# Down projections: a third weight block added in flight, and the seventh product's sums fetched later

## The chip, the cores and the metric

The kernel runs on one core of one Trainium2 chip. Its time is the device time of one execution in microseconds (us), and a smaller time is better. A profiled execution adds a trace: every instruction of the engines PE (matrix products; its weight loads are shown as PEld), DVE, ACT and POOL, the issues of the DMA queue SP, and the transfers' landings. Times inside the trace count from the start of its span.

## What is computed

One decoder layer on 512 rows of 1024 float32 values:

```python
x = x + 0.5 * swiglu(rmsnorm(x, ffn1_norm), ffn1_wg, ffn1_wu, ffn1_wd)
x = x + hybrid_mixer(rmsnorm(x, mix_norm), ...)     # sparse attention beside a gated recurrence
x = x + 0.5 * swiglu(rmsnorm(x, ffn2_norm), ffn2_wg, ffn2_wu, ffn2_wd)
return rmsnorm(x, final_norm)

def swiglu(x, w_gate, w_up, w_down):
    return (jax.nn.silu(x @ w_gate) * (x @ w_up)) @ w_down
```

The inner width of both feed-forward parts is 2816, so each down projection multiplies 512 x 2816 by 2816 x 1024. The change touches only the two down projections.

## The kernel before

Every float32 operand is split into a rounded part and a remainder, and each product is made of three matmuls. For weights this is `wsplit`: ACT writes the rounded part `wh`, and DVE subtracts it from the source to get the remainder `wl`. A step of PE cannot begin before both are there. The tiles `wh` and `wl` have three buffers each, and each holds the split weights of two steps, so the split of a step is placed four steps ahead of the step that uses it.

Of the 22 row blocks of a down weight, six (`PLAIN`) are multiplied directly. The other 16 form eight pairs (`PAIRS`), and for them the kernel uses a Strassen-like scheme with seven products instead of eight. Products 1, 2 and 4 multiply a block of the weight as it is. Products 5, 6, 3 and 7 multiply sums of two, three or four blocks, and these sums of weights are made anew in each execution:

- the sum for product 5 is block 2 + block 3,
- for product 6 it is block 2 + block 3 + block 0,
- for product 3 it is all four blocks,
- for product 7 it is block 2 + block 0.

The first three live one after the other in the same tile `sums[j]`: once product 5's split has read it, a block is added for product 6, and once that split has read it, another is added for product 3. In the first down projection these tiles are called `sm` in the profile, in the second they are the tiles `x`. Product 7's sums have tiles of their own, `s3[j]`, shown as `s`.

A sum is made in two ways. An *adding transfer* is a DMA issued by POOL (`G.dma_start(..., accum_op=ALU.add)`), which adds a block from memory to what the tile holds. The other way, used before for product 6 alone, fetches the block into a tile `a1` (shown as `a`, one of the four buffers of the pool `tmp`) through the queue SP, and DVE adds the two tiles.

`block_down` writes the order of the work out by hand. `steps` is the list of 68 steps of PE, and `task(i, f)` puts the function `f` behind the products of step `i`:

| steps | what |
|---|---|
| 0 to 5 | direct products of the first output half, k = 0 to 5 |
| 6 to 13, 14 to 21, 22 to 29 | products 1, 2 and 5 for the pairs j = 0 to 7 |
| 30 to 39 | product 6, with direct steps of the second half at 33 and 37 |
| 40 to 49 | product 3, with direct steps at 43 and 47 |
| 50 to 57, 58 and 59 | product 7, then the last two direct steps |
| 60 to 67 | product 4 |

A direct step is 12 matmuls with 512 moving columns. A step of products 1 to 7 is 12 matmuls with 256 columns in the first down projection, and 6 matmuls with 512 columns in the second. Each engine and each DMA queue works through its own instructions in the order in which they were written; the program does not reorder them. A transfer of POOL or SP that waits for a tile therefore holds all later transfers of the same queue.

Between the two feed-forward parts stands the mixer. Its order is not written by hand: a planner (`Plan`) keeps an account of the time of each engine, by a cost for each instruction, and places an instruction when its inputs are due by that account. The account begins with the first down projection (`plan.clear()`), so it takes in that projection's DVE additions and DMA issues too.

Of the kernel before, what the change touches and what calls it, by code (L numbers as in the profile page):

```python
# [12 lines left out]
ALU = mybir.AluOpType  # L13
# [161 lines left out]
def hybrid_kernel(ctx, tc, xt, vec, w1u, w1d, wm, wki, wrg, watt, wrnn, wout, w2u, w2d, gf, out):  # L175
    nc = tc.nc
    plan = Plan()
    V, A = plan.engine("DVE", nc.vector), plan.engine("ACT", nc.scalar)
    G, T = plan.engine("POOL", nc.gpsimd), plan.engine("PE", nc.tensor)
    Q = plan.engine("SP", nc.sync)  # L180
# [16 lines left out]
    def nm(s):  # L197
        cnt[0] += 1
        return f"{s}_{cnt[0]}"

    def slot(dt=F32, name="s"):
        return plan.take("slot", big.tile([P, S], dt, tag="slot", name=nm(name)))

    def work(name="t", cols=S):
        return plan.take("tmp", tmp.tile([P, cols], F32, tag="tmp", name=nm(name)))
# [28 lines left out]
    def wsplit(r, h, l):  # L234
        A.activation(h, r, AF.Copy)
        V.tensor_sub(l, r, f(h))
# [355 lines left out]
    def block_down(hs, wd, sums):  # L592

        d = Down()
        steps = [("D", 0, k) for k in range(PLAIN)] + [(p, j) for p in (1, 2, 5) for j in range(PAIRS)]  # L600
        for p in (6, 3):
            for j in range(PAIRS):
                steps += [(p, j)] + [("D", 1, (6, 3).index(p) * 2 + j // 3)] * (j in (2, 5))
        steps += [(7, j) for j in range(PAIRS)] + [("D", 1, k) for k in (4, 5)] + [(4, j) for j in range(PAIRS)]
        index = {s: i for i, s in enumerate(steps)}
        tasks = {}

        def task(i, *fs):
            tasks.setdefault(i, []).extend(fs)

        def block(b, j):

            i, half = b * (PAIRS // 2) + j // 2, j % 2 * S
            return wd[i][:, half:half + S]

        units, turned, ra, raws, s3, ones = {}, {}, {}, {}, {}, {}

        def fetch(key, i):
            def load():
                raws[key] = raw.tile([P, WMAX], F32, tag="raw", name=nm("wr"))  # L620
                Q.dma_start(raws[key], wd[i])

            return load

        def unit(i, src):
            def split_():
                if i % 2 == 0:
                    units[i // 2] = [wsp.tile([P, WMAX], F32R, tag=t, name=nm(t)) for t in ("wh", "wl")]
                wsplit(src(), *(t[:, i % 2 * S:(i % 2 + 1) * S] for t in units[i // 2]))

            return split_

        a = lambda j: hs[PLAIN + 2 * j]
        b = lambda j: hs[PLAIN + 2 * j + 1]

        def differences(j):
            def subs():
                if j % 2 == 0:
                    ra[j // 2] = slot(F32, "cr")
                V.tensor_sub(ra[j // 2][:, (lo, hi)[j % 2]], a(j)[:, hi], b(j)[:, hi])  # L640
                V.tensor_sub(a(j)[:, hi], a(j)[:, hi], a(j)[:, lo])

            return subs

        SRC = {1: lambda j: a(j)[:, lo], 5: lambda j: a(j)[:, hi], 6: lambda j: a(j)[:, lo], 3: lambda j: b(j)[:, hi],
               7: lambda j: ra[j // 2][:, (lo, hi)[j % 2]], 4: lambda j: a(j)[:, lo], 2: lambda j: b(j)[:, lo]}

        def operand(p, j):
            def make():
                o, src = slot(F32R, "cm"), SRC[p](j)  # L650
                turned[p, j] = o
                sign = -1.0 if p in (1, 3) else 1.0
                A.activation(o[:, lo], src, AF.Copy, scale=sign)
                if sign < 0:
                    V.scalar_tensor_tensor(o[:, hi], src, -1.0, f(o[:, lo]), op0=ALU.mult, op1=ALU.subtract)
                else:
                    V.tensor_sub(o[:, hi], src, f(o[:, lo]))

            return make

        used = []
        for i, st in enumerate(steps):
            if st[0] == "D":
                _, h, k = st
                key = ("D", h, k // 2)
                if k % 2 == 0:
                    used.append([i - 4, index["D", h, k + 1] - 4, key, 2 * PAIRS + h * (PLAIN // 2) + k // 2])
                task(i - 4, unit(i, lambda key=key, k=k: raws[key][:, k % 2 * S:(k % 2 + 1) * S]))
                continue
            p, j = st  # L670
            if p in (1, 4, 2):
                key = (p, j // 2)
                if j % 2 == 0:
                    used.append([i - 4, index[p, j + 1] - 4, key, {1: 0, 2: 1, 4: 3}[p] * (PAIRS // 2) + j // 2])
                src = lambda key=key, j=j: raws[key][:, j % 2 * S:(j % 2 + 1) * S]
            elif p == 7:
                src = lambda j=j: s3[j]
            else:
                src = lambda j=j: sums[j]
            if p == 1:  # L680
                task(j, differences(j))
            if p == 5:
                def base(j=j):
                    Q.dma_start(sums[j], block(2, j))

                def add(j=j):
                    G.dma_start(sums[j], block(3, j), accum_op=ALU.add)

                task(3 * j // 2 + 2, base)
                task(3 * j // 2 + 4, add)  # L690
            if p == 7:
                def base(j=j):
                    s3[j] = slot(F32, "s3")
                    Q.dma_start(s3[j], block(2, j))

                def add(j=j):
                    G.dma_start(s3[j], block(0, j), accum_op=ALU.add)

                task(i - 27, base)
                task(i - 25, add)  # L700
            if p == 6:
                def one(j=j):
                    ones[j] = work("a1")
                    Q.dma_start(ones[j], block(0, j))

                def second(j=j):
                    V.tensor_add(sums[j], sums[j], ones[j])

                task(i - 9, one)
                task(i - 5, second)  # L710
            if p == 3:
                def fourth(j=j):
                    G.dma_start(sums[j], block(1, j), accum_op=ALU.add)

                task(index[6, j] - 3, fourth)
            before = {1: 6, 6: 6, 7: i - j - 1, 4: i - index[3, j]}.get(p, 5)
            if p == 6:
                task(i - before - 1, lambda j=j: V.tensor_sub(a(j)[:, lo], b(j)[:, hi], a(j)[:, hi]))
            if p == 4:
                task(i - before - 1, lambda j=j: V.tensor_sub(a(j)[:, lo], b(j)[:, lo], a(j)[:, lo]))  # L720
            task(i - before, operand(p, j))
            task(i - 4, unit(i, src))
        used.sort()
        for n, (first, last, key, i) in enumerate(used):
            at = first - 5
            if n >= RAWS:
                at = max(at, used[n - RAWS][1])
            assert at < first
            task(at, fetch(key, i))

        def tasks_at(i):
            for t in tasks.pop(i, ()):
                t()

        d.steps, d.index, d.tasks, d.tasks_at, d.units, d.turned = steps, index, tasks, tasks_at, units, turned
        return d
# [52 lines left out]

    sums = []  # L790
    d1 = block_down(hs, w1d, sums)
    ffn_up(y, w1u, 2, hs, V_G1, ((WP[0], WP[1]), (WP[2], pu)), AH[1:], d1.tasks_at)

# [77 lines left out]
    steps, index, last = d1.steps, d1.index, len(d1.steps) - TAIL  # L871
# [689 lines left out]


    d2 = block_down(hs, w2d, x)
    steps, index, units, turned, tasks_at = d2.steps, d2.index, d2.units, d2.turned, d2.tasks_at
    xr = []
# [210 lines left out]
```

## Time and profile before

| | |
|---|---|
| median of 3 runs | 1078.01 us (1077.62 to 1078.6) |
| the profiled execution, its own time | 1076.99 us |
| its span in the trace | 1074.9 us |
| granted clock of TensorE, mean | 0.998 |
| PE busy | 1063.3 us, 99% of the span |
| DVE busy | 857.6 us, 80% |
| ACT busy | 657.5 us, 61% |
| POOL busy | 140.8 us, 13% |

The profiled execution is 1.02 us below the median, and 2.09 us of its time lie outside the span. The first down projection takes the stretch from about 235 to 350 us, the second that from about 946 us to the end. Matmuls overlap in the trace: one with 512 columns is shown as 0.39 us long but the next begins 0.23 us after it. So the busy share of PE hides short waits, and the distance between the starts of matmuls shows them.

### The profile page before, as it was taken

The page shows a single profiled execution, that of the slowest core. Times are in us where ns is not written, and L with a number is a line of the kernel's source. Part 1 is how long each engine was busy: PE and PEld are TensorE (multiplying, and loading weights), DVE is VectorE, ACT ScalarE, POOL GpSimd, SP SyncE. Part 2 cuts the span into 40 slices and gives each one's busy share as a digit, 9 for nine tenths or more (in the row PEclk, how much of TensorE's full clock was granted, in tenths as well). Part 3 has the DMA queues.
Part 4 walks back from the last instruction along what each step waited for, and adds up shares of the span by engine and source line. Part 5 has one row for each costly group of instructions (what it writes and reads, how often), then busy time and mean ns, then how long its engine had stood idle before and what let it go on. Part 6 is the DMA issues. An engine that isn't in the chain of part 4 may idle for free.

```text
span 1074.9 us, 17584 instructions
## 1 busy us (share of the span) xinstructions
PE 1063.3 (99%) x6412; PEld 945.4 (88%) x6412; DVE 857.6 (80%) x1668; ACT 657.5 (61%) x1297; POOL 140.8 (13%) x171
## 2 busy tenths in 40 slices
PE   9999999999999999999999999999999999999997
PEld 7889999999989778888888888888899999998776
DVE  6687777779988878998899867666878777778886
ACT  6565655555556658877896664345755555565563
POOL 0161111102320000000000000002511111101310
PEclk9999999999999999999999999999999999999999
DMA  7297677639983442332232213434977777549953
GB/s 276 65 255 194 162 190 196 165 110 242 238 196 118 139 124 83 94 98 79 79 99 82 76 38 86 131 99 128 236 181 192 166 190 191 123 133 285 231 134 118
DMA packets 71702, 161.79 MB, mean 151 GB/s; under 512 B 8512, under 2 KB 14784, under 8 KB 71616
## 3 DMA queue, kind: packets, MB, share of 16 engines
q1 hardware_dynamic: 48912, 123.92, 35.5%
q0 software_dynamic: 22272, 36.19, 20.5%
q8 instruction: 50, 0.82, 0.3%
q10 hardware_dynamic: 432, 0.57, 0.1%
q14 instruction: 36, 0.29, 0.1%
HBM read 151.73 MB, written 2.10 MB: 143 GB/s over the span
## 4 chain that ended last, share of the span: by engine, by line
PE 87%; DMA 6%; DVE 4%; ACT 2%; issue 1%; SPq 0%; POOL 0%; POOLq 0%; ACTq 0%; DVEq 0%
PE mm L169 60%; PE aux L169 26%; DVE wl L169 1%; DMA sm<-w1d 1%; DMA x<-w2d 1%; DMA s<-w2d 1%; DMA s<-w1d 1%; ACT wh L169 1%; DMA cm<-cb 1%; DMA x<-xt 0%; DMA wr<-w1u 0%; DVE yl L169 0%; DVE yf L169 0%; DVE ca L169 0%; ACT cm L169 0%
## 5 line engine op out<-in xcount | busy, mean ns | idle before, releaser
L169 PE MATMUL mm<-cm,wh 128*128 128x256 f32 x1472 | 268.6, 283 | 0.5 <-ACT wh L169 0.5
L169 DVE TENSOR_TENSOR wl<-wr,wh 128x512 fp32r<-128x512 f32 (+2 forms) x228 | 188.9, 832 | 77.9 <-ACT wh L169 77.0
L169 PEld LDWEIGHTS mm<-cm,wh 128*128 128x128 f32 x1472 | 230.1, 192 | 1.4 <-ACT wh L169 0.7
L169 PE MATMUL mm<-cm,wl 128*128 128x256 f32 x736 | 208.5, 283 | 0.2 <-DVE wl L169 0.2
L169 ACT ACTIVATE wh<-wr 128x512 fp32r<-128x512 f32 (+3 forms) x230 | 167.9, 737 | 62.1 <-issue 21.1
L169 PE MATMUL mm<-yh,wh 128*128 128x512 f32 (+1 forms) x416 | 164.2, 396 | 0.4 <-ACT wh L169 0.2
L169 PE MATMUL mm<-yl,wh 128*128 128x512 f32 (+1 forms) x416 | 162.5, 391 | 0.8 <-DVE yl L169 0.8
L169 PE MATMUL aux<-cm,wh 128*128 128x256 f32 x880 | 161.8, 283 | 0.1
L169 PE MATMUL mm<-yh,wl 128*128 128x512 f32 x408 | 159.3, 390 | 0.0
L169 PEld LDWEIGHTS mm<-cm,wl 128*128 128x128 f32 x736 | 141.3, 192 | 0.5 <-DVE wl L169 0.4
L169 PEld LDWEIGHTS aux<-cm,wh 128*128 128x128 f32 x880 | 137.3, 192 | 0.3 <-DMA cm<-cb 0.3
L169 PE MATMUL aux<-cm,wl 128*128 128x256 f32 x440 | 124.5, 283 | 0.0
L169 DVE TENSOR_TENSOR wl<-s,wh 128x512 fp32r<-128x512 f32 x152 | 104.0, 686 | 23.6 <-ACT wh L169 21.6
L169 ACT ACTIVATE wh<-s 128x512 fp32r<-128x512 f32 x152 | 92.5, 623 | 38.9 <-DVE s L169 30.9
L169 PEld LDWEIGHTS mm<-yh,wh 128*128 128x128 f32 (+1 forms) x416 | 77.9, 187 | 17.2 <-ACT wh L169 1.1
L169 PEld LDWEIGHTS mm<-yl,wh 128*128 128x128 f32 (+1 forms) x416 | 77.6, 187 | 16.9 <-DVE yl L169 2.2
L169 PEld LDWEIGHTS mm<-yh,wl 128*128 128x128 f32 x408 | 76.6, 188 | 16.5 <-DVE wl L169 0.2
L169 PEld LDWEIGHTS aux<-cm,wl 128*128 128x128 f32 x440 | 84.5, 192 | 0.0
L169 PE MATMUL mm<-wh,cm 128*128 128x512 f32 x192 | 59.6, 392 | 1.2 <-ACT wh L169 1.1
L169 ACT ACTIVATE tg<-mm 128x256 f32<-128x256 f32 x68 | 26.1, 384 | 52.8 <-PE mm L169 52.6
L157 POOL DMA_DIRECT2D cm<-cb x8 | 7.1, 886 | 334.6 <-DMA wr<-w2u 280.1
L157 POOL DMA_DIRECT2D s<-w2u x36 | 33.6, 1092 | 127.5 <-DMA s<-w2u 92.1
(243 smaller groups left out, 2016.8 us busy)
## 6 DMA issues: line engine op xcount, KB each, us to landing
wr<-wm SPq DMA_DIRECT2D x39, 512.0 KB, 3.5
wr<-w2u SPq DMA_DIRECT2D x26, 512.0 KB, 4.9
wr<-w1u SPq DMA_DIRECT2D x21, 512.0 KB, 5.9
wr<-w1d SPq DMA_DIRECT2D x18, 512.0 KB, 4.2
s<-w2u SPq DMA_DIRECT2D x36, 256.0 KB, 5.9
s<-w2u POOLq DMA_DIRECT2D x36, 256.0 KB, 5.0
wr<-w2d SPq DMA_DIRECT2D x18, 512.0 KB, 4.7
s<-w1u SPq DMA_DIRECT2D x32, 256.0 KB, 6.2
```

Of the source, the lines that this page charges most:

```text
L157: return self.engine.dma_start(out, src, **kw)
L169: return call(*args, **kw)
```

## The change

Three things are edited in `block_down`, and they act in both down projections:

- Product 6's third block is no longer fetched into `a1` and added by DVE. It is an adding transfer of POOL into `sums[j]`, written one step behind product 5's split of the same tile (step 19 + j) where the addition stood five steps ahead of product 6's step.
- Product 7's two transfers into `s3[j]` move from 27 and 25 steps ahead of its step to 14 and 12 ahead. The order on POOL's queue becomes: all eight additions for 6, all eight for 3, all eight for 7. Before, those for 7 alternated with those for 3.
- The dictionary `ones` and the tile `a1` go.

```diff
-        units, turned, ra, raws, s3, ones = {}, {}, {}, {}, {}, {}
+        units, turned, ra, raws, s3 = {}, {}, {}, {}, {}
...
                 def add(j=j):
                     G.dma_start(s3[j], block(0, j), accum_op=ALU.add)
 
-                task(i - 27, base)
-                task(i - 25, add)
+                task(i - 14, base)
+                task(i - 12, add)
             if p == 6:
-                def one(j=j):
-                    ones[j] = work("a1")
-                    Q.dma_start(ones[j], block(0, j))
-
                 def second(j=j):
-                    V.tensor_add(sums[j], sums[j], ones[j])
-
-                task(i - 9, one)
-                task(i - 5, second)
+                    G.dma_start(sums[j], block(0, j), accum_op=ALU.add)
+
+                task(index[5, j] - 3, second)
             if p == 3:
                 def fourth(j=j):
                     G.dma_start(sums[j], block(1, j), accum_op=ALU.add)
```

In each down projection SP loses eight fetches, DVE loses eight additions, and POOL's queue gets eight transfers more.

## The prediction

> **What bounds the kernel now.** The page comes first: its span and busy times.
>
> ```profile
> span 1074.9 us, 17584 instructions
> PE 1063.3 (99%) x6412; PEld 945.4 (88%) x6412; DVE 857.6 (80%) x1668; ACT 657.5 (61%) x1297; POOL 140.8 (13%) x171
> ```
>
> PE is the bound, so only time in which PE falls behind its own pace can be won. The pace is read next, in the timeline of PE, at the starts of direct steps (`aux<-hh` or `aux<-wh,hh`). First down projection, steps 33, 37, 43 and 47:
>
> ```profile
> 290.53 0.40 PE L169 MATMUL aux<-hh,wh 128*128 128x512 f32 x1
> ...
> 297.59 0.40 PE L169 MATMUL aux<-hh,wh 128*128 128x512 f32 x1
> ...
> 307.53 0.40 PE L169 MATMUL aux<-hh,wh 128*128 128x512 f32 x1
> ...
> 315.99 0.40 PE L169 MATMUL aux<-hh,wh 128*128 128x512 f32 x1
> ```
>
> From 33 to 37, one direct step and three others take 7.06 us. From 37 to 43, with five others, it is 9.94, so two others cost 2.88: 1.44 each, 2.74 for the direct one. From 43 to 47 stands the mix of the first stretch again, and it takes 8.46: PE loses 1.40 there. Second projection, steps 30, 33, 37, 43 and 47:
>
> ```profile
> 1003.81 0.62 PE L169 MATMUL mm<-wh,cm 128*128 128x512 f32 x2
> ...
> 1008.20 0.40 PE L169 MATMUL aux<-wh,hh 128*128 128x512 f32 x1
> ...
> 1016.61 0.39 PE L169 MATMUL aux<-wh,hh 128*128 128x512 f32 x1
> ...
> 1026.16 0.39 PE L169 MATMUL aux<-wh,hh 128*128 128x512 f32 x1
> ...
> 1035.06 0.39 PE L169 MATMUL aux<-wh,hh 128*128 128x512 f32 x1
> ```
>
> All matmuls have 512 columns here. From 37 to 43 stand 12 + 5 x 6 = 42 of them in 9.55 us, 0.227 each, which I take as the pace. The stretch from 30 to 33 (18 matmuls, 4.09) takes 4.39, from 33 to 37 (30 matmuls, 6.82) 8.41, from 43 to 47 (30 again) 8.90. The losses are 0.30, 1.59 and 2.08, 3.97 together. Both projections lose 1.40 + 3.97 = 5.37 us, in products 6 and 3 alone. What ends these waits is told by the timeline of ACT, whose last bracket is the idle time and its releaser:
>
> ```profile
> 1005.75 0.63 ACT L169 ACTIVATE wh<-x 128x512 fp32r<-128x512 f32 x1 [1.44 <-DVE x L169]
> ...
> 1030.00 0.63 ACT L169 ACTIVATE wh<-x 128x512 fp32r<-128x512 f32 x1 [1.50 <-DMA x<-w2d]
> ```
>
> ```profile
> 313.28 0.63 ACT L169 ACTIVATE wh<-sm 128x512 fp32r<-128x512 f32 x1 [1.46 <-DMA sm<-w1d]
> ```
>
> In product 6 of the second projection ACT waits for DVE's addition. With the addition 0.69 long, the rounding 0.63 and the subtraction 0.69,
>
> ```profile
> 1004.95 0.69 DVE L169 TENSOR_TENSOR x<-x,a 128x512 f32<-128x512 f32 x1
> ...
> 1006.42 0.69 DVE L169 TENSOR_TENSOR wl<-x,wh 128x512 fp32r<-128x512 f32 x1 [0.44 <-ACT wh L169]
> ```
>
> a block goes DVE, ACT, DVE in 2.01 us, longer than the 1.36 (6 x 0.227) of the step that it feeds. In product 3 the adding transfer itself lands late. Why is seen on POOL:
>
> ```profile
> 1021.10 0.87 POOL L157 DMA_DIRECT2D s<-w2d  x1 [2.24 <-DMA s<-w2d]
> 1021.63 3.01 POOL L157 DMA_DIRECT2D x<-w2d  x3
> ```
>
> The last three additions for product 3 (`x`) go out only after an addition for product 7 (`s`), which had to wait for its own base block. The windows of the two stages show the engines that carry the change:
>
> ```profile
> 300.00:319.00 19.00, 18.25 (x126) 16.70 (x125) 14.70 (x35) 10.91 (x25) 4.10 (x6) 1.00 0.90 212
> 319.00:334.00 15.00, 15.00 (x124) 14.87 (x123) 14.35 (x29) 11.40 (x22) 1.55 (x3) 1.00 0.19 55
> ...
> 1006.00:1020.00 14.00, 13.78 (x55) 9.44 (x54) 11.80 (x23) 6.27 (x13) 6.72 (x8) 1.00 1.06 256
> 1020.00:1035.00 15.00, 14.04 (x58) 10.38 (x58) 11.19 (x24) 8.45 (x21) 3.55 (x4) 1.00 1.01 228
> 1035.00:1052.00 17.00, 17.00 (x76) 14.05 (x76) 16.93 (x36) 11.26 (x25) 0.00 (x0) 1.00 0.17 59
> ```
>
> The columns are the stretch, its length, busy time of PE, PEld, DVE, ACT and POOL, PE's clock, the DMA engines' share and GB/s. The clock is 1.00 throughout, so there is none to win. DMA is full until product 7 begins and then nearly idle.
>
> **The change part by part.** *DVE's additions go.* Eight of 0.69 us in each projection, 5.5 us of DVE work, of which PE feels only the chain above: 0.30 + 1.59 = 1.89 us in the second projection. In the first, product 6 already runs at pace, so nothing is won there.
>
> *The addition becomes a transfer.* It has to land before ACT and DVE split the block. It can go out once DVE has read the tile for product 5. The first and the last of these eight subtractions in each projection:
>
> ```profile
> 271.94 0.68 DVE L169 TENSOR_TENSOR wl<-sm,wh 128x512 fp32r<-128x512 f32 x1
> ...
> 280.83 0.68 DVE L169 TENSOR_TENSOR wl<-sm,wh 128x512 fp32r<-128x512 f32 x1
> ```
>
> ```profile
> 990.89 0.69 DVE L169 TENSOR_TENSOR wl<-x,wh 128x512 fp32r<-128x512 f32 x1
> ...
> 999.75 0.69 DVE L169 TENSOR_TENSOR wl<-x,wh 128x512 fp32r<-128x512 f32 x1
> ```
>
> First projection: out at 272.6. Step 30 begins three steps before 290.53, at 286.2; a split of 0.63 + 0.68 makes 284.9 the last moment. That is 12.3 us. Second: from 991.6 to 1003.81 - 1.3 = 1002.5, 10.9 us. The eighth has 19 us in both (281.5 to 300.5; 1000.4 to 1019.4). The trace has no such transfer at this place; the nearest are the adding transfers of the same stages, and below them those of the second up projection:
>
> ```profile
> sm<-w1d POOLq DMA_DIRECT2D x16, 256.0 KB, 8.2
> ```
>
> ```profile
> x<-w2d POOLq DMA_DIRECT2D x16, 256.0 KB, 9.0
> ...
> s<-w2d SPq DMA_DIRECT2D x8, 256.0 KB, 9.2
> s<-w2d POOLq DMA_DIRECT2D x8, 256.0 KB, 9.9
> ```
>
> ```profile
> s<-w2u POOLq DMA_DIRECT2D x36, 256.0 KB, 5.0
> ```
>
> Medians from issue to landing are 8.2 and 9.0 at the upper end, 5.0 at the lower. All are under 10.9, so no wait takes the place of the old one. I expect about 6, because the sixteen fetches for products 6 and 7 that shared those moments are gone or later.
>
> New waits: POOL stands still until DVE's subtraction has read the tile. Behind it on POOL are only more additions, which need the same tiles later, so nobody else pays. The cost is nothing; if that cover went, it would be the lateness of the last rival.
>
> *The additions for product 3* no longer stand behind those for product 7. Each goes out when product 6's split of its tile is done, nine steps ahead of its own split, and I book the whole losses there, 1.40 and 2.08 us, as won. What could come late next are product 7's own sums.
>
> *Product 7's sums* start at step 36. In the second projection step 36 begins at 1003.81 + 42 x 0.227 = 1013.3 and step 50 is 102 matmuls later, at 1036.5: 23.2 us for base, addition and split. At the crowded medians that is 9.2 + 9.9 + 1.3 = 20.4. For j = 7 (step 43 to 57, 96 matmuls) there are 21.8. It fits, by 1.4 to 2.8 us. SP has lost the fetches into four `a1` buffers that made it wait for DVE; the fetches left on it are for later steps.
>
> *DMA work.* The queues' shares over the first projection's 130 us:
>
> ```profile
> q1 hardware_dynamic: 6591, 17.33, 41.4%
> q0 software_dynamic: 3648, 6.82, 28.4%
> ```
>
> The plain queue takes 0.414 x 130 / 17.33 = 3.1 us of all engines for each MB, the adding one 0.284 x 130 / 6.82 = 5.4. For 0.262 MB that is 0.81 and 1.42 us, so eight changed transfers add 4.9 us of DMA work in each projection. The stretch after 319 has 0.81 x 15 = 12.2 us free, and product 7's transfers (16 in each) move towards it; I price the extra work at nothing. The Trainium skill, "DMA: Bandwidth & Descriptors", section "Issuing engines are not separate DMA queues", says that transfers from all queues run on the same 16 engines and interleave. By this rule, which speaks against the change, the sum would be that of the last rival below, 1082.4, instead of 1072.3. The trace agrees with it as far as the engines are full (1.06, 1.01), and differs in that they are so only until product 7.
>
> *The mixer is re-planned.* The planner's account no longer holds the DVE additions, so its order shifts by a few instructions. At its start the norm's row sums on PE stand three matmuls later (0.68 us). One `wl` moves ahead of the first `yf`, into DVE's idle time, and the subtraction for `VV` moves behind the last `yl`:
>
> ```profile
> 359.12 0.75 DVE L169 SCALAR_TENSOR_TENSOR yf<-x,vt,rstd 128x512 f32<-128x512 f32 x1 [3.05 <-ACT rstd L169]
> ...
> 360.39 1.22 DVE L169 TENSOR_TENSOR wl<-wr,wh 128x1024 fp32r<-128x1024 f32 x1
> ...
> 381.35 0.42 DVE L169 TENSOR_TENSOR VV<-aux,VV 128x256 fp32r<-128x256 f32 x1
> ```
>
> ```profile
> 384.17 0.51 PE L169 MATMUL mm<-yl,wh 128*128 128x512 f32 x1 [0.77 <-DVE yl L169]
> ```
>
> DVE works almost without a pause from the first `yf` to the `yl` for which PE waits, so that chain gets 1.22 + 0.42 - 0.68, about 1 us, shorter, and the wait of 0.77 can go. The rest of the reordering has no row; I bound it by 1 us to either side and book 0.3 us won in all.
>
> **Sum.** 1.89 + 1.40 + 2.08 + 0.3 = 5.7 us. The profiled execution, 1076.99, becomes 1071.3, its span 1069.2. The median of the runs stands 1.02 above the profiled one, so the forecast is 1072.3.
>
> **Rivals.** *Product 7 comes late.* For: its sums start 13 steps later, with the spare of 1.4 us. If base and addition took 11.5 us each, 23 with 20.5 to spend (21.8 - 1.3), j = 7 would be 2.5 us late in the second projection, and in the first, where two direct steps and twelve others make 22.8, 1.5 us: 4 us back, 1076.3. Against: the crowd of transfers that made these medians is spread out.
>
> *The planner takes it back.* The mixer has some 300 us of reordered work. If it cost 4 us, the time would be 1076.6. Against: PE waits little in the mixer now, and the one large wait gets shorter.
>
> *The wait only changes its name,* from ACT's wait for DVE to one for the transfer. If the new additions took 13.5 us, PE would be held 1.2 us at step 30 of the first projection and 2.6 us in the second: 1076.1. For: ACT is the engine that waits now. Against: it takes a landing half as long again as the crowded median of 9.0.
>
> *Slower: DMA is the bound,* as the rule above has it. The engines stay full until 1035, and the extra 4.9 us in each projection lands on PE's path. Then 5.4 are won and 9.8 lost: 1082.4. It needs landings over 15.6 us: with 12.3 and 10.9 us of cover, each us beyond costs 2 us, and it takes 8 us to lose 5.7 and 0.2% more. For: the longest landing in the first projection,
>
> ```profile
> DMA to landing us min/median/max: 3.8/7.0/15.2
> ```
>
> of the tiles `sm`, is close. Against: that one stood behind the alternating queue.
>
> **How the numbers follow.** 0.2% (2.2 us, up to 1075.85) is about what can be told from no change. The forecast, with all that comes out between 1070.3 and 1075: 0.78. Product 7 late 0.05, planner 0.06, the renamed wait 0.05; their prices lie at the edge of what can be told apart, so somewhat under half of these 0.16 counts as faster (0.07) and the rest as same (0.09). DMA as the bound: 0.06, slower. That makes faster 0.85, same 0.09, slower 0.06. The range goes from 1070.3, with 1 us more from the mixer and one from the other small waits, to 1076.0, which leaves out the DMA bound and about half of the three cases at the edge.
>
> **What would show it.** Steps 33 to 37 at 6.8 us and 43 to 47 at 7.06 and 6.8; no `DVE x` or `DMA x` as releaser of ACT there; the additions landing after 5 to 8 us; DMA above 0.5 in the stretch that shows 0.19. The prediction is wrong if ACT waits for `DMA x` at step 30, if product 7's `wh<-s` waits for `DMA s`, or if the mixer is longer by more than 1 us.

## The result, and the profile after

The changed kernel takes 1073.83 us (median of 6 runs, 1073.08 to 1074.89), the kernel before 1077.82 (6 runs, 1076.39 to 1078.6): a ratio of 0.9965, with a 95% interval of 0.9952 to 0.9977. That is about 4 us faster, where 5.7 were forecast. The profiled execution is a run of 1073.98 us, and its page begins:

```profile
span 1071.9 us, 17576 instructions
...
PE 1060.3 (99%) x6412; PEld 947.9 (88%) x6412; DVE 848.8 (79%) x1652; ACT 656.3 (61%) x1295; POOL 153.8 (14%) x187
```

DVE has 8.8 us less to do, POOL 13 more, and PE still sets the time. First the stretches that the prediction named, in PE's timeline: steps 43 and 47 of the first projection, then 33, 37, 43 and 47 of the second.

```profile
307.41 0.40 PE L169 MATMUL aux<-hh,wh 128*128 128x512 f32 x1
...
314.47 0.40 PE L169 MATMUL aux<-hh,wh 128*128 128x512 f32 x1
```

```profile
1008.67 0.39 PE L169 MATMUL aux<-wh,hh 128*128 128x512 f32 x1
...
1015.47 0.39 PE L169 MATMUL aux<-wh,hh 128*128 128x512 f32 x1
...
1024.99 0.39 PE L169 MATMUL aux<-wh,hh 128*128 128x512 f32 x1
...
1031.79 0.39 PE L169 MATMUL aux<-wh,hh 128*128 128x512 f32 x1
```

They take 7.06, 6.80 and 6.80 us, exactly what the prediction asked for: PE loses nothing there any more. On POOL the last of product 3's additions (`x`) now goes out ahead of the first of product 7's (`s`):

```profile
1013.48 1.76 POOL L157 DMA_DIRECT2D x<-w2d  x2 [1.51 <-DVE wl L169]
1014.77 2.25 POOL L157 DMA_DIRECT2D s<-w2d  x2
```

Part of what came back was lost again in the mixer. PE's timeline where the attention ends and the jobs on its halves (`ath`, `atl`) begin, before:

```profile
653.02 0.39 PE L169 MATMUL mm<-rh,wl 128*128 128x512 f32 x1
653.25 0.39 PE L169 MATMUL mm<-ath,wh 128*128 128x512 f32 x1
```

and after:

```profile
649.94 0.39 PE L169 MATMUL aux<-ptl,VV 128*128 128x512 f32 x1
651.53 0.50 PE L169 MATMUL mm<-ath,wh 128*128 128x512 f32 x1 [1.20 <-ACT ath L169]
652.97 0.50 PE L169 MATMUL mm<-atl,wh 128*128 128x512 f32 x1 [0.93 <-DVE atl L169]
...
654.24 0.63 PE L169 MATMUL mm<-ath,wh 128*128 128x512 f32 x1
654.67 0.63 PE L169 MATMUL mm<-atl,wh 128*128 128x512 f32 x1
```

Before, recurrent jobs (`rh`) filled PE while ACT and DVE split the attention's result. After, those matmuls have been issued earlier, the last attention product is followed at once by the job that needs the split, and PE waits. Then the starts are 0.43 us apart instead of 0.23: the windows (stretch, length, busy PE, PEld, DVE, ACT, POOL, PE's clock, DMA share, GB/s) show the clock at 0.57 there.

```profile
650.00:654.00 4.00, 1.86 (x7) 1.04 (x6) 2.92 (x7) 3.20 (x6) 0.00 (x0) 1.00 0.00 0
654.00:658.00 4.00, 4.00 (x12) 3.14 (x11) 2.24 (x5) 0.63 (x1) 0.00 (x0) 0.57 0.27 66
```

To place every microsecond, I summed over all matmuls of a trace the distance from one start to the next, less the median distance of that form. Losses of PE by stage, in us, from one trace of each kernel (e1 to e12 are the experiments below; in e7 and e8 matmuls that fill a wait don't count as lost). The medians come from several sessions, in which the kernel before took 1077.1 to 1077.8 us; each ratio below is to its executions in the same session.

| kernel | first down projection (303 to 321) | mixer (360 to 720) | second down projection (982 to 1038) | median time |
|---|---|---|---|---|
| before | 1.43 | 3.82 | 4.44 | 1077.82 |
| after | 0.03 | 6.59 | -0.08 | 1073.83 |
| e1: after's transfers, before's mixer order | 0.03 | 3.73 | 0.00 | 1070.97 |
| e2: before's transfers, after's mixer order | 1.25 | 6.62 | 5.26 | 1078.74 |
| e3: product 7 later alone | 0.03 | 3.70 | 1.91 | 1073.64 |
| e4: adding transfers alone | 1.53 | 3.73 | 5.98 | 1077.83 |
| e7: after, eleven matmuls fill the wait | 0.03 | 2.45 | 0.70 | 1072.42 |
| e8: after, five | 0.03 | 3.88 | 0.30 | 1072.29 |
| e10: after, R7 ahead of A0 | 0.03 | 2.15 | -0.08 | 1069.12 |
| e12: before, R7 ahead of A0 | 0.91 | 3.75 | 6.00 | 1076.93 |

From before to after the down projections gain 1.40 + 4.52 = 5.9 us, and the mixer loses 2.8 more: 4.34 more from the last attention product (649.94 us) to 720, where the attention is split, 1.6 less elsewhere. The difference of the spans is 3.0.

### The profile page after: what moved, and what is told of

Its sections match the earlier page's. It is cut to its first block, busy times and chain, and to the rows that moved or that the text cites. A ratio compares the mean times of both kernels' runs of the same rounds, so it can differ in the third digit from the quotient of the medians.

```text
span 1071.9 us, 17576 instructions
## 1 busy us (share of the span) xinstructions
PE 1060.3 (99%) x6412; PEld 947.9 (88%) x6412; DVE 848.8 (79%) x1652; ACT 656.3 (61%) x1295; POOL 153.8 (14%) x187
## 4 chain that ended last, share of the span: by engine, by line
PE 91%; DVE 4%; ACT 2%; issue 1%; DMA 1%; SPq 0%; ACTq 0%; DVEq 0%
PE mm L169 64%; PE aux L169 28%; DVE wl L169 1%; ACT wh L169 1%; DVE ca L169 1%; SPq L157 0%; DMA x<-xt 0%; ACT cm L169 0%; DVE yl L169 0%; DVE h L169 0%; DVE yf L169 0%; DVE cb L169 0%; ACT tg L169 0%; DVE cm L169 0%; ACT yh L169 0%
## 5 line engine op out<-in xcount | busy, mean ns | idle before, releaser
L169 PE MATMUL aux<-cm,wh 128*128 128x256 f32 x880 | 161.5, 283 | 0.0
L157 POOL DMA_DIRECT2D cm<-cb x8 | 7.1, 884 | 337.7 <-DMA wr<-w2u 283.3
L157 POOL DMA_DIRECT2D s<-w2u x36 | 33.5, 1067 | 126.6 <-DMA s<-w2u 109.6
```

The source lines that it names most:

```text
L157: return self.engine.dma_start(out, src, **kw)
L169: return call(*args, **kw)
```

## The experiments

My theory A was that the gain is the change's own and the new loss is an accident of the mixer's order, which the planner makes from an account in which the changed transfers stand. The rival B was that the loss comes of reaching the mixer earlier, or of the transfers.

**e1 and e2: the transfers and the order taken apart.** In e1 the new transfers are issued past the account, and the account gets the old entries at the old steps:

```
-                    Q.dma_start(s3[j], block(2, j))
+                    nc.sync.dma_start(s3[j], block(2, j))
...
+                def base_account(j=j):
+                    plan.copy(held7[j], block(2, j), "SP")
...
+                task(i - 27, base_account)
+                task(i - 25, add_account)
...
+                    plan.add("DVE", 0.07 + S / 960, (sums[j],), (sums[j], held6[j]))
```

PE and ACT then run in the order of before, instruction by instruction; DVE too, but for the additions left out. e2 is the mirror image.

> The changed kernel, but the planner's account of its transfers is that of the kernel before (entries for the old base fetch, the old third fetch and the old DVE addition at their old steps, nothing for the new ones), so that every engine's order in the mixer is the one of before. Theory A, that the gain in the down projections is the change's own and the loss at the split of attention (PE waits of 1.36 and 1.21 us and then 3.4 us at half clock) comes from the new mixer order: the down projections lose nothing against PE's pace, as in the changed kernel, the mixer loses 4.3 us as before instead of 7.0, no half clock between the projections, 1073.8 - 2.7 = 1071.1 us. Rival B, that the loss at the split comes from reaching the mixer 1.4 us earlier or from the transfers themselves, whatever the order: 1073.8 us with the half clock at 654 us still there.

> The kernel before, but the planner's account is that of the changed kernel, so that the mixer runs in the changed kernel's order while the down projections issue their transfers and DVE additions as before. Theory A (the loss is of the order): the down projections lose 5.9 us as before, the mixer 7.0 us with a half clock of about 3.4 us behind the split of attention, 1077.8 + 2.7 = 1080.5 us. Rival B (the loss is of the earlier arrival or of the transfers): 1077.8 us, full clock.

e1 took 1070.97 us, 0.9942 [0.9929, 0.9954] of before, against 1071.1 expected. No wait and full clock at the split:

```profile
650.00:652.00 2.00, 2.00 (x11) 1.65 (x10) 2.00 (x4) 0.63 (x1) 0.00 (x0) 1.00 0.50 131
652.00:654.00 2.00, 2.00 (x11) 1.65 (x10) 1.35 (x4) 0.23 (x1) 0.00 (x0) 1.00 0.00 0
```

e2, with nothing changed in the down projections, has the wait and the slow matmuls:

```profile
652.66 0.50 PE L169 MATMUL mm<-ath,wh 128*128 128x512 f32 x1 [1.20 <-ACT ath L169]
654.09 0.50 PE L169 MATMUL mm<-atl,wh 128*128 128x512 f32 x1 [0.93 <-DVE atl L169]
...
655.20 0.63 PE L169 MATMUL mm<-atl,wh 128*128 128x512 f32 x1
```

The loss is of the order; B falls. But e2's median is 1078.74, 1.0011 [1.0003, 1.0019] of before, so 1.2 us and not 2.7. The twelve executions differ: five with a mean clock of 0.997 took 1079.0 to 1080.5 (mean 1079.8; the profiled one is among them), seven with 0.998 or 0.999 took 1076.4 to 1079.6 (mean 1077.7). It fits that the half clock follows the wait in some executions only; the single ones were not traced, so that is argued, not shown.

Which entries make the new order follows from the programs alone. With product 7's entries at their old steps and product 6's new ones, PE, DVE (without the additions) and ACT stand in the order of before; with product 6's old entries and product 7's new ones, in the order of after. The moved fetch does it. Adding up the account's entries shows how. With product 7's new entries alone its PE waits 1.7 us longer (149.1 instead of 147.4 us at the mixer's start), and its DVE stands 5.6 instead of 4.7 us behind PE there. Product 6's new entries bring its PE to 161.5 us, but leave that distance at 4.7, and the order with it. The trace shows no such wait of PE.

**e3 and e4: each half alone,** with the account and the mixer order of before. e3 moves only product 7's two fetches (`i - 27` to `i - 14`, `i - 25` to `i - 12`), e4 only replaces the fetch and the DVE addition of product 6 by the adding transfer.

> Half of the change: the seventh product's sums fetched later (14 and 12 steps ahead), the sixth product's third block still fetched and added on DVE; planner's account and mixer order of before. Theory A (product 3's stall comes from its additions standing behind product 7's on POOL): the stalls in front of product 3 go, 1.43 us in the first projection and 2.10 us in the second, those of product 6 (1.93 us in the second) stay, 1077.8 - 3.5 = 1074.3 us. Rival C, that one stall covers the other and what is freed at product 3 was slack that product 6 gives back: the second projection's loss stays near 4 us, 1076.4 us.

> The other half: the sixth product's third block as an adding transfer, the seventh product's sums still fetched 27 and 25 steps ahead; planner's account and mixer order of before. Theory A (each half takes its own stall): product 6's 1.93 us in the second projection go, product 3's 1.43 and 2.10 us stay since its additions still stand between product 7's on POOL, 1077.8 - 1.9 = 1075.9 us. Rival D, that product 6's new additions now stand behind product 7's waiting ones too: they land later than needed, and the time is 1077.8 us or more.

e3: 1073.64 us, 0.9965 [0.9953, 0.9978]; A's 1074.3 was near, and what stays is product 6's 1.9 us. ACT still waits for DVE, and product 7's additions leave in a row, behind all of product 3's:

```profile
1012.84 0.63 ACT L169 ACTIVATE wh<-x 128x512 fp32r<-128x512 f32 x1 [1.44 <-DVE x L169]
```

```profile
1019.83 0.86 POOL L157 DMA_DIRECT2D x<-w2d  x1 [1.13 <-DVE wl L169]
1020.37 6.57 POOL L704 DMA_DIRECT2D s<-w2d  x7
```

e4: 1077.83 us, 1.0006 [0.9997, 1.0014]: nothing, where A said 1.9 us. D had the time right, but not which additions come late. PE at steps 33, 37, 43 and 47 of the second projection:

```profile
1007.92 0.39 PE L169 MATMUL aux<-wh,hh 128*128 128x512 f32 x1
...
1014.72 0.39 PE L169 MATMUL aux<-wh,hh 128*128 128x512 f32 x1
...
1027.24 0.39 PE L169 MATMUL aux<-wh,hh 128*128 128x512 f32 x1
...
1036.22 0.40 PE L169 MATMUL aux<-wh,hh 128*128 128x512 f32 x1
```

Product 6 runs at pace (6.80 us from 33 to 37): its stall is gone, as A said. But the next stretches take 12.52 and 8.98 us instead of 9.5 and 6.8, so product 3's stall grows from 2.1 to 5.2. POOL and ACT show why:

```profile
1002.87 0.86 POOL L157 DMA_DIRECT2D s<-w2d  x1 [1.02 <-DMA x<-w2d]
1005.67 0.87 POOL L157 DMA_DIRECT2D x<-w2d  x1 [1.94 <-DMA x<-w2d]
```

```profile
1022.19 0.63 ACT L169 ACTIVATE wh<-x 128x512 fp32r<-128x512 f32 x1 [3.34 <-DMA x<-w2d]
```

Product 7's additions (`s`) still stand between product 3's (`x`, L157) on POOL, and eight more transfers now pass the same line ahead of them. The line is full: in none of the traces does POOL have more than eight transfers on their way, and at 1005.67 us the next one leaves only when another has landed. Over a whole execution, 36 of POOL's issues find seven others on their way in e4, 18 in after and 7 in before. So the adding transfers bring 1.9 us of PE's time (e3 to e1; 2.7 between the medians) behind the moved fetches, and without them product 3 loses at least what product 6 wins.

**e5 and e6: how much cover the new additions have.** e1 with `index[5, j] - 1` and `index[5, j] + 1` in place of `index[5, j] - 3`.

> As the kernel with the old account (e1), but the sixth product's additions are issued two steps later (one step before the fifth product's step instead of three), 2.7 us in the second projection. Theory A (an addition lands a fixed 7 to 11 us behind its issue, and PE has 1.5 to 2.8 us in hand): a stall of about 1 us in front of product 6 in the second projection, and nothing in the first, where the additions have more in hand: 1071 + 1 = 1072.0 us. Rival B (what sets the landing is the line of additions, which land no closer than 1.25 us to each other whenever they are issued): under 0.5 us, 1071.2 us.

> The same, four steps later (one step behind the fifth product's step), 5.4 us in the second projection. Theory A (fixed 7 to 11 us): 2.6 to 3.9 us of stall in the second projection and 2.7 to 4 us more in the first, if its margin is no larger, 1074 to 1078 us. Rival B (the line of additions): the first additions of product 6 land 5 us later but the later ones hardly, 1 to 2 us in all, 1072.5 us.

1071.06 and 1070.91 us: no loss in either. My premise was wrong, since a step sets only the place in POOL's queue, and POOL doesn't run by PE's steps. In e1 the additions for j = 4 to 7 leave at 994.24 to 998.16 (L718), in e6 those for j = 5 to 7 only behind product 3's first (L157):

```profile
994.24 1.80 POOL L718 DMA_DIRECT2D x<-w2d  x2 [1.26 <-DVE wl L169]
996.45 0.86 POOL L718 DMA_DIRECT2D x<-w2d  x1 [0.41 <-DVE wl L169]
998.16 0.86 POOL L718 DMA_DIRECT2D x<-w2d  x1 [0.85 <-DVE wl L169]
```

```profile
1000.18 0.87 POOL L157 DMA_DIRECT2D x<-w2d  x1 [4.66 <-DVE wl L169]
1000.71 1.22 POOL L718 DMA_DIRECT2D x<-w2d  x1
...
1003.51 1.99 POOL L718 DMA_DIRECT2D x<-w2d  x1
```

The eighth addition leaves 5.4 us later and lands 4.7 us later (1014.13 against 1009.41), and PE doesn't wait. The line as a whole lands at nearly the same moments, whichever transfer stands in it: 1006.36, 1007.93 and 1009.67 us in e6, 1006.14, 1007.74 and 1009.41 in e1.

**e7 and e8: why the clock halves.** Filling matmuls ahead of the first job on the attention halves, eleven in e7, five in e8:

```
+            if job == "A0":
+                ys[0]
+                for _ in range(11):
+                    nc.tensor.matmul(ps, ws[i][0][:, :P], ws[i][0][:, :S], start=True, stop=True)
```

> The changed kernel with eleven additional matmuls (128x512, on the weights of the job, overwritten by the job's own first one) right in front of the first job on the attention halves, which fill 2.5 us in which PE waits there. Theory A (the half clock from 654.2 to 657.6 us comes from these waits): the waits are filled and the job starts no later, the clock stays full, 1.7 us less, 1073.8 - 1.7 = 1072.1 us. Rival B (the clock falls for another reason): half clock still there, 1073.8 us or more.

> The same with five additional matmuls, which fill 1.13 us of the first wait and leave the second (0.93 us idle). Theory A (only the sum of the two waits is long enough): full clock, 1072.1 us. Theory A2 (the second wait alone is enough): half clock for 3.4 us, 1073.8 us. Rival B (another reason): half clock, 1073.8 us; it goes with A2 here and is told from it by the run with eleven.

1072.42 and 1072.29 us (0.9949 of before in both), 1.4 and 1.5 less than after, and the clock is full in both traces. The windows of e7, then of e8, whose second wait is still there:

```profile
650.00:654.00 4.00, 4.00 (x18) 3.06 (x18) 3.04 (x8) 3.20 (x6) 0.00 (x0) 1.00 0.00 0
654.00:658.00 4.00, 4.00 (x20) 3.29 (x19) 2.80 (x5) 1.27 (x2) 0.00 (x0) 1.00 0.21 70
```

```profile
650.00:654.00 4.00, 3.00 (x13) 1.92 (x12) 3.43 (x8) 3.05 (x6) 0.00 (x0) 1.00 0.00 0
654.00:658.00 4.00, 4.00 (x19) 3.33 (x18) 2.78 (x5) 1.44 (x3) 0.00 (x0) 1.00 0.24 67
```

So the half clock comes of PE's idleness, as far as one trace of each shows: 0.93 us of it is too little, 1.20 and 0.93 within 3 us are enough.

**e9: more transfers in the line.** e1 with `task(index[5, j] - 3, second, *[second] * (j < 4))`.

> As the kernel with the old account (e1), but the sixth product's addition is issued twice for j below 4, four adding transfers of 256 KB more in each down projection (the sums of those blocks hold block 0 twice). Theory A (the line of additions lands one every 1.25 to 2.0 us and is nearly as fast as it must be): all later landings move by 4 x 1.25 = 5 to 4 x 2 = 8 us, PE has 2 to 3 us in hand, so 2 to 5 us of stall in the second projection and 0 to 4 in the first, 1073 to 1080 us, likeliest 1075. Rival B (the line has room, its spacing is that of the issues): under 1 us, 1071 to 1072 us.

1103.78 us, 1.0244 [1.0227, 1.0262]: 33 us more, far outside both. It doesn't measure the room in the line, because I put the two additions to one tile next to each other, and the second is issued only when the first has landed. All of POOL's queue stands behind it:

```profile
1021.89 1.75 POOL L718 DMA_DIRECT2D x<-w2d  x2 [5.14 <-DMA x<-w2d]
1028.32 1.75 POOL L718 DMA_DIRECT2D x<-w2d  x2 [4.68 <-DMA x<-w2d]
```

Each pair costs some 6.4 us, and PE loses 14.6 and 18.5 us in the two projections, in part at half clock: behind these waits the clock is halved for 27 us in all (290.0 to 303.6, 1020.4 to 1030.7 and 1034.1 to 1037.5 us). What the line can still take stays open. It does show what the changed kernel avoids: there the additions to one tile stand several other transfers apart on POOL.

**e11: the price of adding.** e1 with `accum_op=ALU.add` left out of the down projections.

> As the kernel with the old account, but the 32 adding transfers of each down projection are plain copies onto the same tiles (the sums hold the last block alone). Theory A (adding costs the line 1.42 us of engine time per 256 KB where a plain copy takes 0.81): landings come as close as 0.8 us and their mean distance in the second projection falls from 1.7 us, the latency of 7 to 12.5 us falls to 4 to 6; no time for the program, 1071.0 us, since PE has no stall there. Rival B (the distance is that of the queue's own issue, 0.86 to 0.93 us on POOL plus its waits, not of the addition): landings stay 1.25 to 1.7 us apart.

1070.50 us, 0.9935 [0.9919, 0.9952], not to be told from e1. The DMA issues between 986 and 1038 us (the last column is the median from issue to landing), of e1 and of e11:

```profile
x<-w2d POOLq DMA_DIRECT2D x17, 256.0 KB, 11.0
s<-w2d SPq DMA_DIRECT2D x8, 256.0 KB, 7.6
s<-w2d POOLq DMA_DIRECT2D x8, 256.0 KB, 11.9
```

```profile
x<-w2d POOLq DMA_DIRECT2D x16, 256.0 KB, 4.0
s<-w2d SPq DMA_DIRECT2D x8, 256.0 KB, 4.2
s<-w2d POOLq DMA_DIRECT2D x8, 256.0 KB, 7.4
```

In a full line plain copies land 0.66 us apart (e11, 1016.89 to 1022.87 us), adding ones some 1.3 (e1, 1022.08 to 1027.21). A was right: the adding makes the latency, and PE pays none of it.

**e10 and e12: a version that beats both.** In the mixer's list of jobs R7 stands in front of A0:

```
-R4 R5 R6 A0 A1 A2 A3 A4 A5 R7 A6 A7 O0 O1 O2 O3 O4 O5 O6 O7
+R4 R5 R6 R7 A0 A1 A2 A3 A4 A5 A6 A7 O0 O1 O2 O3 O4 O5 O6 O7
```

> The changed kernel with its own planner's account, and in the list of the mixer's jobs the last recurrent job, R7, stands in front of the first job on the attention halves (R6 R7 A0 ... A6) instead of between A5 and A6, so that 5.4 us of matmuls lie between the last attention product and A0. Theory A (the changed kernel's loss at 650 us is PE without work while the halves are split): the two waits of 1.36 and 1.21 us and the half clock's 1.7 us go, 4.3 us, against which A6 and the output jobs lose their cover, 0 to 1.5 us: 1069.5 us (1069.5 to 1071), under e1's 1071.0. Rival B (what R7 covered between A5 and A6 is worth as much, by the wait for the last split of the sums): 1072 to 1074 us.

> The kernel before with R7 in front of A0 as in e10, nothing else. Theory A (R7's place only repairs what the changed kernel's order broke; before had 4 us of recurrent matmuls between the last attention product and A0 and lost nothing there): no difference, 1077.3 us (1076.8 to 1078), with the down projections losing 5.9 us as before. Rival B (R7's new place is worth something by itself, so that e10's time doesn't show what the split had cost): 1075 us or less.

e10 took 1069.12 us, 0.9920 [0.9905, 0.9935] of before, the fastest of all; e12, the same edit in the kernel before, 1076.93, 0.9998 [0.9988, 1.0008]. The list repairs what the new order broke and is worth nothing where nothing was broken. That e10 is below e1 too comes from the new order, which loses 1.6 us less elsewhere in the mixer (2.15 us in all against 3.73). PE in e10, where R7 covers the split:

```profile
651.09 0.39 PE L169 MATMUL aux<-ptl,VV 128*128 128x512 f32 x1
651.32 0.39 PE L169 MATMUL mm<-rh,wh 128*128 128x512 f32 x1
...
655.40 0.39 PE L169 MATMUL mm<-ath,wh 128*128 128x512 f32 x1
```

## Why the prediction was right, and where it wasn't

The forecast was 1072.3 us, the result 1073.8, inside the range and on the side that was given 0.85. The parts of the sum did not all hold, and that the total came within 1.5 us of the forecast is in part luck: the spans of the two traces are 3.0 us apart, little more than half of the 5.7 booked, and the medians 4.0.

*Product 3, 1.40 + 2.08 us:* right, in place, size and cause. e3 takes 3.5 us off by moving product 7's fetches alone.

*Product 6, 0.30 + 1.59 us:* right in size (1.93 in the trace), but booked as standing by itself. e4 shows that it is kept only with product 7's fetches moved: without that, product 3 loses at least as much more.

*Not booked:* 0.42 us in the second projection between 982 and 994. It goes in after, but is 0.00 to 0.84 in the experiments' traces, so I count it as chance.

*The mixer, 0.3 us won within 1 us:* this is the step that failed. It came to 2.8 us lost in the trace, and so one of the prediction's own signs of being wrong, a mixer longer by more than 1 us, came true. The one wait with a row of its own went as forecast, from 0.77 to 0.17 us:

```profile
381.98 0.50 PE L169 MATMUL mm<-yl,wh 128*128 128x512 f32 x1 [0.17 <-DVE yl L169]
```

The rest was bounded by 1 us without a row, and it was the rest that paid. The rival named "the planner takes it back" had the mechanism and 0.06 of the chance; its counter-argument, that PE waits little in the mixer, was read from the very order that the change replaces. The reason given was wrong too: the DVE additions' entries don't move the order, product 7's do, and DVE stands later behind PE in the account, not earlier.

*The landing of the new additions, 5 to 8 us:* wrong; product 6's eight of the second projection took 7.3 to 11.3 us, with three to six others on their way ahead of them. No wait of PE came of it. In after, the tightest is j = 2, landed at 1003.73 us; its step is six matmuls before the direct one at 1008.67, so at 1007.31, less 1.3 for the split: 2.3 us in hand. But "no `DMA x` as releaser of ACT" did not hold:

```profile
1003.84 0.63 ACT L169 ACTIVATE wh<-x 128x512 fp32r<-128x512 f32 x1 [1.09 <-DMA x<-w2d]
...
1009.02 0.63 ACT L169 ACTIVATE wh<-x 128x512 fp32r<-128x512 f32 x1 [0.92 <-DMA x<-w2d]
```

ACT waits for the transfer, and PE, fed four steps ahead, doesn't notice. That ACT waited was no sign of a loss, and I had made it one.

*Product 7, a spare of 1.4 to 2.8 us:* too small. Its first base fetch left at 989.83 us, 24 before step 36 (1014.1), as soon as PE had released SP's wait for a tile (`PE aux` by the trace), and its last sum landed at 1037.59 us, 7.8 before the last moment for its split (1045.4: step 47 at 1031.79, and 66 matmuls later step 57, less 1.3). The step in the task list was read as a time, the same mistake as in e5 and e6.

*DMA as the bound:* it was not. The engines stay full until product 7 begins and have room behind it, if less than the "above 0.5" that was to be seen in the last stretch:

```profile
1017.00:1032.00 15.00, 15.00 (x67) 12.41 (x67) 12.28 (x28) 9.04 (x21) 5.20 (x7) 1.00 1.10 248
1032.00:1049.00 17.00, 17.00 (x76) 14.08 (x75) 13.83 (x27) 8.98 (x19) 0.00 (x0) 1.00 0.46 98
```

Together: 5.4 booked and 5.9 won in the down projections, 0.3 booked and -2.8 got in the mixer. The median's 1.02 us above the profiled run, which the forecast added, was -0.15 in after.

## What to carry to other kernels

Where a planner orders later work by an account of earlier work, an edit to the earlier work is also an edit to the later order: compare the two programs' orders engine by engine, look for each place where a filler has left the gap that it filled, and book a microsecond or more for it rather than a few tenths. Put a movable job directly behind the last product of a chain whose result has to be split before PE can go on. A transfer's place in a task list says what it stands behind in its queue, not when it leaves, and a half of an edit can be worth nothing until the other half has cleared that queue.

## What the hardware showed that was not expected

PE's clock halved from 654.2 to 657.6 us, 3.4 us, after two waits with 1.20 and 0.93 us idle, neither of them long; e8, with the second wait alone, kept the full clock. The waits cost 2.6 us and the clock some 1.7 more, two thirds again. The Trainium skill, "TensorE: Matmul & The Clock Gate", Part 1, has the clock set from free-running windows of about 3.4 us, which agrees with the length of the slow stretch and would fit the spread of e2's executions; its section "Why this matters for your kernels" advises to leave no gap over some 3 us between bursts of matmuls; here the longest gap was 1.20 us, and the trace decides.

An adding transfer of 256 KB takes some 1.3 us of a full line (e1) where a plain copy takes 0.66 (e11), and the line's backlog makes most of the 10 us from issue to landing. With seven ahead of it, an addition waits for eight landings, 8 x 1.3 = 10.4 us by these spacings; in after, product 7's first left behind seven others at 1014.77 us and landed at 1027.29.
